# Six of the first pair's sixteen on-chip moves put on ScalarE's queue, and the remainders of the last two combinations of x put on VectorE, the last combination started after the first scores

## The chip, the cores and the metric

The kernel runs on one core of one Trainium2 chip. The metric is device time in microseconds (us), of one launch that computes both layers. Times of single instructions come from a profile of one execution.

## What is computed

The reference is a two-layer encoder block over x of shape (1, 512, 1024), in float32. Each layer is RMSNorm, one input projection, a token mixer with per-head RMS-normed queries and keys, a product with silu(gate), an output projection and a residual add.

```python
def reference(x, ...):
    for i in range(DEPTH):                       # 2 layers
        hn = rms_norm(x, norm_gain[i])
        if i % 2 == 0:
            y = mixer_a(hn, a_w_in, a_w_out, a_q_gain, a_k_gain, t5_bias)
        else:
            y = mixer_b(hn, b_w_in, b_w_out, b_q_gain, b_k_gain, b_rpb)
        x = x + y

def mixer_a(hn, w_in, w_out, q_gain, k_gain, t5_bias):
    proj = hn @ w_in                             # 1024 -> 3 groups * (q, k, v) * 1024, and a gate
    for g, (window, dilation) in enumerate(((128, 1), (512, 4), (2048, 16))):
        o, lse = dilated_group_attention(rms_norm(q), rms_norm(k), v, bias, dilation, reach)
    y = sum over g of softmax(lse)[g] * o[g]     # the three groups share one softmax
    return (y * silu(gate)) @ w_out
```

`mixer_b` is neighbourhood attention on an 8 x 64 grid. The change touches layer A alone, and in it the first pair of heads and the preparation of x.

## The kernel before

**Matrix products.** Every float32 operand is split into a high part that TensorE takes in its fast float32 form (`..._h`, `wh`) and a remainder (`..._l`, `wl` = value minus high part); a product is three matmuls. ScalarE makes the high parts of the weights (`cast`), VectorE and GpSimd take turns at the remainders (`rest`). Weights come through eight `wraw` buffers, and there are six `wh` and five `wl` buffers.

**Layer A's projections.** The sixteen heads are worked in eight pairs, `hc` = 0 to 7. Pairs 1 to 7 form their projections with fewer products, as in Strassen's scheme: `main_a(hc)` multiplies quarters of x with four sums of weight blocks, and, for that, four combinations of the quarters of x are made once, in `mix()`. `mix()` makes combination n in three steps (`put(n, ...)`): a VectorE sum or difference into the buffer `mixed`, a ScalarE copy into `mix_h[:, n]`, and a subtraction into `mix_l[:, n]`, on the engine that `put` is given. All are [128 x 1024]. They are made in the order 0, 1, 3, 2, and the products of `main_a` ask for them in that order too (`yield "mix", n`). Combination 2 is used last, behind the second scores of the first pair.

**Attention of a pair** is `attn_a(hc)`. `scores(u)`, u = 0 and 1, gives four [128 x 512] tiles each; `least` puts on each a VectorE minimum, a ScalarE exponential (`exponents`), a ScalarE scaling (`normalise`) and a VectorE transposition into `pq` (`turn`; buffer name `pt`). When the eight tiles of the pair are in `pq`, sixteen DMAs of 64 KB move [32 x 512] blocks from `pq` to another buffer, `t0` (also printed `pt`), in which the rows stand in the order that the local group's product needs: `move(n)`, n = 0 to 3, issues four of them, all on SyncE's queue. Each reads columns that all eight transpositions write. `weigh()` then gives the output `o` in 128 small matmuls `o<-pt,rawk`, which read `pq` itself, and 64 matmuls `o<-pt,v`, which read `t0` and so wait for the moves. `weighed` multiplies it with the gate.

**Order.** TensorE's order is written out by hand. A main stream of products and a side stream of attention work are interleaved by a planner's clock, `clock`, in ns: it adds up what each matmul should take (213 ns for 512 columns). `yield "wait", key, delay` holds the side stream until that clock is `delay` past the time put into `stamp[key]`; `yield key` makes the main stream run the side stream until the key is there; `later_on(delay, job)` sets work off when the clock has gone on by `delay`. Inside `in_order()`, and in `keep_in_program_order(...)`, work keeps the written order on its engine; the rest of VectorE's, ScalarE's, GpSimd's and SyncE's order comes from a scheduler at build time. At run time each engine works off its own list strictly in order, and a DMA that SyncE issues waits, at the head of SyncE's list, for its data.

Around the change the order by the planner's clock is: `put(3)` at 47.8 us, `put(2)` at 52.9, keys transposed (`k_a(0)`) from 61.0, first scores at 64.5, second scores at 74.9, moves from 84.7 to 88.6, `weigh` at 93.5.

Of the kernel before, what the change touches and what calls it, by code (L numbers as in the profile page):

```python
# [13 lines left out]
F32 = mybir.dt.float32  # L14
# [8 lines left out]
P = 128  # L23
# [3 lines left out]
NHC = 8  # L27
# [19 lines left out]
def tile_hybrid_encoder(  # L47
# [19 lines left out]
    wk = ctx.enter_context(tc.tile_pool(name="wk", bufs=2))  # L67
# [22 lines left out]
    @contextmanager  # L90
    def in_order():

        was, held[0] = held[0], True
        yield
        held[0] = was

    vec, act, pol, syn = (Ordered(e) for e in (nc.vector, nc.scalar, nc.gpsimd, nc.sync))

    def sb(t, off, dims):
        return bass.AP(t.tensor, t.offset + off, [t.ap[0]] + dims)  # L100
# [13 lines left out]
    def bank(name):  # L114

        return ps_side.tile([P, 512], F32, tag="side", name=name)
# [18 lines left out]
    mix_h = big.tile([P, 4, 4, H], F32R, tag="yh", name="mix_h")  # L135
    mix_l = big.tile([P, 4, 4, H], F32R, tag="yl", name="mix_l")
# [180 lines left out]
    stamp = {("qk", -1): 0, ("w", -1): 0}  # L317
# [26 lines left out]
    def later_on(delay, job):  # L344

        timers.append((clock[0] + delay, job))
        timers.sort(key=lambda t: t[0])
# [120 lines left out]
    pq = wk.tile([P, 4096], F32, tag="pt", name="pt", bufs=1)  # L468
# [57 lines left out]
    def mix():  # L526


        x11, x12, x21, x22 = (x_all[:, k : k + KH, t : t + H] for t in (0, H) for k in (0, KH))
        t = wk.tile([P, 2, KH, H], F32, tag="tr", name="mixed", bufs=1)  # L530
        a, b = t[:, 0], t[:, 1]

        def put(n, out, op, x, y, eng):
            with in_order():
                op(out, x, y)
                act.copy(mix_h[:, n], out)
                eng.tensor_sub(mix_l[:, n], out, mix_h[:, n].bitcast(F32))
            stamp["mix", n] = 0

        yield "wait", ("first",), 500  # L540
        yield from first_out()
        yield 1500
        put(0, a, vec.tensor_sub, x21, x22, pol)
        yield 2000
        put(1, b, vec.tensor_sub, a, x11, vec)
        yield 2000
        yield from bias_lines()
        yield "wait", ("rawk", 0), 1000
        put(3, b, vec.tensor_add, b, x12, pol)
        yield 5000  # L550
        put(2, a, vec.tensor_sub, x11, x21, pol)

    def row_sums(ssq):

# [5 lines left out]
    def bias_lines():  # L560

        oh = wk.tile([32, 896], F32, tag="k12", name="oh", bufs=1)
        tc.keep_in_program_order(syn.dma_start(oh, onehot))
        t5 = wk.tile([32, 48], F32, tag="e0", name="t5", bufs=1)
        syn.dma_start(t5, t5t)
        mk = wk.tile([16, 896], F32, tag="q12", name="mk", bufs=1)
        syn.dma_start(mk, maskc)
        yield 3000
        for g, (o, n) in enumerate(((0, 384), (384, 256), (640, 256))):
            pl = bank("pl")  # L570
            matmul(pl[0:16, :n], t5[:, 16 * g : 16 * g + 16], oh[:, o : o + n], start=True, stop=True)
            vec.tensor_sub(mk[:, o : o + n], mk[:, o : o + n], pl[0:16, :n])
        for j in range(4):
            syn.dma_start(l0_d[:, j, j : j + 384], mk[:, 0:384])
        syn.dma_start(l12_d, mk[:, 384:896])
        yield
# [77 lines left out]
    def first_out():  # L654

        raw, ss = st.pop("first")
        for i in range(4):
            t = raw[:, i, :]
            act.activation(t, t, AF.Copy, scale=rs_n[:, i : i + 1])
            squares(t, ss, i, 8)  # L660
            yield 0
        normed(raw, ss, 8, "rawq", 0)
# [242 lines left out]
    class turner:  # L905
# [7 lines left out]
        def put(self, src, n, off):  # L913

            dst = sb(self.t, off, [[32, n // P], [self.run, 4], [1, 32]])
            vec.transpose(dst, src[:, :n].rearrange("p (i b k) -> p i b k", b=4, k=32))
# [21 lines left out]
    def attn_a(hc):  # L938
# [1 line left out]
        q0h, q0l, q12, k0h, k0l = st.pop(("q", hc))  # L940
        k12, v12 = st.pop(("k12", hc))
        last = hc == NHC - 1
        t0 = pq if last else wk.tile([P, 2048], F32, tag="tr", name="pt0", bufs=1)
        run = 1024 if last else 512
        moved = []
        at = lambda t, hd: 32 * (4 * hd + t)
# [4 lines left out]
            src = pr[:, 512 - P * n : 512]  # L951
            vec.transpose(dst, src.rearrange("p (i b k) -> p i b k", b=4, k=32))

        def move(n):

            place = t0.rearrange("p (a x) -> p a x", a=4)
            for b in range(4):
                a = (b + n) % 4
                src = pq[32 * a : 32 * a + 32, 1024 * b : 1024 * b + 512]
                tc.keep_in_program_order(syn.dma_start(place[32 * b : 32 * b + 32, a, :], src))  # L960
            moved.append(n)
            if len(moved) == 4:
                stamp["pt", hc] = clock[0]

        def scores(u):

            tiles = []
            for t in (2 * u, 2 * u + 1):
                cs, n = (64, 192) if t == 0 else (0, 192) if t == 3 else (0, 256)
                tiles.append((t, [bank("log") for _ in range(2)], cs, n))  # L970
            for t, lgs, cs, n in tiles:
                ks = slice(P * t + cs, P * t + cs + n)
                qs = slice(P * t, P * t + P)
                mm3_heads(
                    [lg[:, cs : cs + n] for lg in lgs],
                    lambda hs: q0h[hs, qs], lambda hs: q0l[hs, qs],
                    lambda hs: k0h[hs, ks], lambda hs: k0l[hs, ks], False,
                )
            for t, lgs, cs, n in tiles:
                for g in range(2):  # L980
                    for j in range(4):
                        c = P * t + 32 * j
                        for hd in range(2):
                            hs = slice(64 * hd, 64 * hd + 64)
                            matmul(
                                lgs[hd][32 * j : 32 * j + 32, 256 + P * g : 384 + P * g],
                                q12[hs, g, c : c + 32],
                                by_class(k12[hs, g, :])[:, :, j],
                                share=2,
                                start=False,  # L990
                                stop=(g == 1),
                            )
            return [(hd, t, lgs[hd], cs, n) for t, lgs, cs, n in tiles for hd in range(2)]
# [43 lines left out]
        def weigh():  # L1037
            os, v0 = [bank("o") for _ in range(4)], st.pop("v0")
            mms = []
            for g in range(2):  # L1040
                for b in range(4):
                    for j in range(4):
                        own = slice(32 * j, 32 * j + 32)
                        c, d = P * g, 1024 * b + 256 * (2 + g)
                        mms.append((
                            lambda hs, j=j: os[j][hs, :P],
                            lambda hs, own=own, b=b, c=c: v12[own, b, c + hs.start : c + hs.stop],
                            lambda hd, own=own, d=d: pq[own, d + at(0, hd) : d + at(0, hd) + P],
                        ))
            for i in range(4):  # L1050
                (ta, ia), (tb, ib) = ((i - 1, 1), (i, 0)) if i else ((0, 0), (3, 1))
                n, m = 32 * (tb - ta), 256 * (ib - ia) + 32 * (tb - ta)
                for a in range(4):
                    mms.append((
                        lambda hs, a=a, d=32 * ta, n=n: sb(os[a][hs], d, [[n, 2], [1, 32]]),
                        lambda hs, i=i: v0[:, i, hs],
                        lambda hd, d=run * a + 256 * ia + 32 * ta, m=m: sb(t0, d + 128 * hd, [[m, 2], [1, 32]]),
                    ))
            yield from side_by_side(mms, 4)
            return os  # L1060

        if last:
# [21 lines left out]
            for c in range(4):  # L1084
                src = gt.rearrange("p (t ja x) -> p x ja t", t=4, ja=8)[:, 4 * c : 4 * c + 4]
# [15 lines left out]
        for u in range(2):  # L1101
            for n, tile_ in enumerate(scores(u)):
                later_on(400 + 900 * n, partial(least, n, tile_))
            if u:
                stamp["scored", hc] = 0
                for n in range(4):
                    later_on(8000 + (2000 if hc else 1300) * n, partial(move, n))
            yield 8500
        fill = bias_rows() if hc == 2 else None
        yield from v_a(hc)  # L1110
        yield "wait", ("pt", hc), 2500
        if hc:
            st["e", hc + 1] = bias_a(hc + 1)
        yield "wait", ("pt", hc), (4500, 11500)[hc] if hc < 2 else 9000 if hc == NHC - 2 else 7500
        yield "wait", ("gate", hc), 4000
        gt = weighed(hc, (yield from weigh()))
        if not hc:
# [402 lines left out]
```

## Time and profile before

| | us |
|---|---|
| median of 3 runs | 858.39 (854.2 to 860.99) |
| the profiled execution, its own time | 856.92 |
| its span | 855.1 |
| TensorE matmul busy | 833.6 (97%) |
| VectorE busy | 634.5 (74%) |
| ScalarE busy | 507.5 (59%) |
| GpSimd busy | 296.5 (35%) |

Engines are called PE (TensorE's matmuls), PEld (its weight loads), DVE (VectorE), ACT (ScalarE), POOL (GpSimd) and SP (SyncE); SPq and ACTq are their DMA issues. A row of a timeline has the start in us, the duration in us, the engine, the line, the operation, what it writes and reads, the form, the count, and in brackets how long the engine had been idle and what ended that. Matmuls are pipelined, so the pace is the distance between starts, not the printed duration. L324 and L328 are the lines of the helpers that record matmuls and transpositions, L85 that of all other engines' work.

### The profile page before, as it was taken

The page shows a single profiled execution, that of the slowest core. Times are in us where ns is not written, and L with a number is a line of the kernel's source. Part 1 is how long each engine was busy: PE and PEld are TensorE (multiplying, and loading weights), DVE is VectorE, ACT ScalarE, POOL GpSimd, SP SyncE. Part 2 cuts the span into 40 slices and gives each one's busy share as a digit, 9 for nine tenths or more (in the row PEclk, how much of TensorE's full clock was granted, in tenths as well). Part 3 has the DMA queues.
Part 4 walks back from the last instruction along what each step waited for, and adds up shares of the span by engine and source line. Part 5 has one row for each costly group of instructions (what it writes and reads, how often), then busy time and mean ns, then how long its engine had stood idle before and what let it go on. Part 6 is the DMA issues. An engine that isn't in the chain of part 4 may idle for free.

```text
span 855.1 us, 18125 instructions
## 1 busy us (share of the span) xinstructions
PE 833.6 (97%) x6611; PEld 688.8 (81%) x6611; DVE 634.5 (74%) x1653; ACT 507.5 (59%) x1066; POOL 296.5 (35%) x259
## 2 busy tenths in 40 slices
PE   9998989999999999999999999899999999999998
PEld 6876867878877878878877877689998898889786
DVE  7899895797897787786886866656578666776742
ACT  7566665765855846846846828545456654665440
POOL 5045442362453543543533514113123322322301
PEclk9999999999999999999999999999999999999999
DMA  9425754766676775776675664283264456534212
GB/s 339 138 56 134 206 130 136 144 164 193 136 174 193 159 176 180 161 164 184 157 174 178 126 193 144 80 297 112 81 193 145 124 169 185 158 134 126 84 50 99
DMA packets 56169, 131.97 MB, mean 154 GB/s; under 512 B 7184, under 2 KB 24528, under 8 KB 55952
## 3 DMA queue, kind: packets, MB, share of 16 engines
q1 hardware_dynamic: 49744, 108.78, 40.5%
q0 software_dynamic: 6048, 22.02, 15.0%
q8 instruction: 52, 0.85, 0.4%
q14 instruction: 37, 0.30, 0.1%
q10 hardware_dynamic: 288, 0.01, 0.0%
HBM read 111.73 MB, written 11.72 MB: 144 GB/s over the span
## 4 chain that ended last, share of the span: by engine, by line
PE 70%; ACT 10%; DVE 10%; DMA 5%; issue 3%; SPq 1%; POOL 1%; ACTq 0%; DVEq 0%
PE acc L324 58%; ACT p L85 4%; PE log L324 4%; PE o L324 4%; DMA wraw<-in_w 3%; PE tp L328 3%; DVE wl L85 2%; ACT wh L85 2%; SPq L85 1%; ACT rawk L85 1%; DVE rawq L85 1%; DVE na L85 1%; DMA e<-l_d 1%; DVE p L85 1%; DVE gt L85 1%
## 5 line engine op out<-in xcount | busy, mean ns | idle before, releaser
L85 POOL TENSOR_TENSOR wl<-wraw,wh 128x512 fp32r<-128x512 f32 (+1 forms) x153 | 197.4, 1291 | 425.2 <-PE acc L324 200.2
L85 ACT CAST wh<-wraw 128x512 fp32r<-128x512 f32 (+1 forms) x360 | 209.7, 593 | 198.9 <-PE acc L324 158.2
L85 DVE TENSOR_TENSOR wl<-wraw,wh 128x512 fp32r<-128x512 f32 (+1 forms) x207 | 160.4, 778 | 43.3 <-PE acc L324 33.9
L324 PE MATMUL acc<-wh,hn_h 128*128 128x384 f32 (+1 forms) x488 | 186.7, 383 | 3.0 <-DVE gt L85 1.7
L324 PE MATMUL acc<-wl,hn_h 128*128 128x384 f32 (+1 forms) x488 | 177.5, 364 | 0.4 <-DVE wl L85 0.4
L324 PE MATMUL acc<-wh,hn_l 128*128 128x384 f32 (+1 forms) x488 | 177.5, 364 | 0.0
L85 ACT ACTIVATE p<-p,mn 128x256 f32<-128x256 f32 (+2 forms) x248 | 137.7, 584 | 32.1 <-DVE mn L85 32.1
L324 PEld LDWEIGHTS acc<-wh,hn_h 128*128 128x128 f32 x488 | 92.3, 189 | 21.6 <-issue 6.8
L324 PEld LDWEIGHTS acc<-wh,hn_l 128*128 128x128 f32 x488 | 92.1, 189 | 9.8
L324 PEld LDWEIGHTS acc<-wl,hn_h 128*128 128x128 f32 x488 | 92.6, 190 | 8.5 <-DVE wl L85 1.1
L324 PE MATMUL acc<-wl,mix_h 128*128 128x512 f32 x224 | 88.2, 394 | 2.1 <-DVE wl L85 2.1
L324 PE MATMUL acc<-wh,mix_h 128*128 128x512 f32 x224 | 89.5, 400 | 0.0
L324 PE MATMUL acc<-wh,mix_l 128*128 128x512 f32 x224 | 87.8, 392 | 0.0
L324 PE MATMUL acc<-hn_h,wh 128*128 128x512 f32 x192 | 79.0, 412 | 0.3 <-ACT rawb L85 0.2
L324 PE MATMUL acc<-hn_h,wl 128*128 128x512 f32 x192 | 75.1, 391 | 0.0
L324 PE MATMUL acc<-hn_l,wh 128*128 128x512 f32 x192 | 75.0, 391 | 0.0
L85 DVE STREAM_TRANSPOSE pt<-p 128x512 f32<-128x512 f32 (+1 forms) x60 | 40.6, 687 | 23.7 <-ACT p L85 23.6
L85 DVE TENSOR_REDUCE ss<-sq 128x4 f32<-128x256 f32 (+1 forms) x96 | 46.1, 500 | 11.1 <-POOL sq L85 5.9
L324 PE MATMUL acc<-y_h,wh 128*128 128x512 f32 x128 | 51.9, 405 | 0.5 <-ACT gt L85 0.5
L324 PEld LDWEIGHTS acc<-wl,mix_h 128*128 128x128 f32 x224 | 42.3, 189 | 11.5 <-DVE wl L85 3.3
L324 PEld LDWEIGHTS acc<-wh,mix_h 128*128 128x128 f32 x224 | 42.2, 188 | 10.0 <-issue 1.6
L324 PE MATMUL acc<-y_h,wl 128*128 128x512 f32 x128 | 50.0, 391 | 0.0
(149 smaller groups left out, 1379.8 us busy)
## 6 DMA issues: line engine op xcount, KB each, us to landing
wraw<-in_w SPq DMA_DIRECT2D x95, 512.0 KB
wraw<-in_w POOLq DMA_DIRECT2D x42, 512.0 KB, 7.0
wraw<-in_w SPq DMA_DIRECT2D x38, 384.0 KB
pt<-pt SPq DMA_DIRECT2D x112, 64.0 KB
td<-tr SPq DMA_DIRECT2D x24, 224.0 KB
pt<-td SPq DMA_DIRECT2D x24, 224.0 KB
e<-l_d SPq DMA_DIRECT2D x32, 112.0 KB
e<-l_d SPq DMA_DIRECT2D x16, 128.0 KB
```

The source lines that it names most:

```text
L85: m = f(*args, **kw)
L324: nc.tensor.matmul(o, l, r, **kw)
L328: nc.tensor.transpose(o, i, ident)
```

## The change

`put` is given a delay: with it, the remainder is taken that much later by the planner's clock. The remainders of combinations 3 and 2 go from GpSimd (`pol`) to VectorE (`vec`), 1500 and 3000 ns behind their combination. Combination 2, the last, starts 15000 ns behind combination 3. Because it still uses `mixed` then, the buffer `t0`, which shares its place, is taken at the first move only.

`move` takes a queue and a list of blocks. For the first pair (`hc` = 0) ten of the sixteen moves stay on SyncE's queue, at 8000 to 11000 ns behind the second scores, and six go on ScalarE's, at 12000 to 16500 ns. For the other pairs all stay on SyncE's, with the times as they were. The waits ahead of the first pair's `weigh`, 2500 and then 4500 ns behind the last move, become zero.

```diff
-        def put(n, out, op, x, y, eng):
+        def put(n, out, op, x, y, eng, wait=0):
+            def split():
+                with in_order():
+                    eng.tensor_sub(mix_l[:, n], out, mix_h[:, n].bitcast(F32))
+                stamp["mix", n] = 0
+
             with in_order():
                 op(out, x, y)
                 act.copy(mix_h[:, n], out)
-                eng.tensor_sub(mix_l[:, n], out, mix_h[:, n].bitcast(F32))
-            stamp["mix", n] = 0
+            later_on(wait, split) if wait else split()
...
-        put(3, b, vec.tensor_add, b, x12, pol)
+        put(3, b, vec.tensor_add, b, x12, vec, 1500)
+        later_on(15000, partial(put, 2, a, vec.tensor_sub, x11, x21, vec, 3000))
         yield 5000
-        put(2, a, vec.tensor_sub, x11, x21, pol)
...
-        t0 = pq if last else wk.tile([P, 2048], F32, tag="tr", name="pt0", bufs=1)
+        t0 = [pq] if last else []
...
-        def move(n):
-
-            place = t0.rearrange("p (a x) -> p a x", a=4)
-            for b in range(4):
+        def move(n, queue, bs):
+
+            if not t0:
+                t0.append(wk.tile([P, 2048], F32, tag="tr", name="pt0", bufs=1))
+            place = t0[0].rearrange("p (a x) -> p a x", a=4)
+            for b in bs:
                 a = (b + n) % 4
                 src = pq[32 * a : 32 * a + 32, 1024 * b : 1024 * b + 512]
-                tc.keep_in_program_order(syn.dma_start(place[32 * b : 32 * b + 32, a, :], src))
-            moved.append(n)
-            if len(moved) == 4:
+                tc.keep_in_program_order(queue.dma_start(place[32 * b : 32 * b + 32, a, :], src))
+                moved.append(a)
+            if len(moved) == 16:
                 stamp["pt", hc] = clock[0]
+
+        def moves():
+            if hc:
+                for n in range(4):
+                    later_on(8000 + 2000 * n, partial(move, n, syn, range(4)))
+                return
+            for n in range(4):
+                later_on(8000 + 1000 * n, partial(move, n, syn, (0, 2, 3) if n % 2 else (1, 3)))
+            for i, (n, b) in enumerate(((0, 0), (0, 2), (1, 1), (2, 0), (2, 2), (3, 1))):
+                later_on(12000 + 900 * i, partial(move, n, act, (b,)))
...
-                for n in range(4):
-                    later_on(8000 + (2000 if hc else 1300) * n, partial(move, n))
+                moves()
...
-        yield "wait", ("pt", hc), 2500
+        yield "wait", ("pt", hc), 2500 if hc else 0
         if hc:
             st["e", hc + 1] = bias_a(hc + 1)
-        yield "wait", ("pt", hc), (4500, 11500)[hc] if hc < 2 else 9000 if hc == NHC - 2 else 7500
+        yield "wait", ("pt", hc), (0, 11500)[hc] if hc < 2 else 9000 if hc == NHC - 2 else 7500
```

More of the change, by code (lines that the diff above doesn't have):

```diff
@@ L1056, in weigh @@
                         lambda hs, i=i: v0[:, i, hs],
-                        lambda hd, d=run * a + 256 * ia + 32 * ta, m=m: sb(t0, d + 128 * hd, [[m, 2], [1, 32]]),
+                        lambda hd, d=run * a + 256 * ia + 32 * ta, m=m: sb(t0[0], d + 128 * hd, [[m, 2], [1, 32]]),
                     ))
```

## The prediction

> **What bounds the kernel now.** I read the page first, then TensorE's waits, then the timeline of each engine around the waits that stand out.
>
> ```profile
> span 855.1 us, 18125 instructions
> PE 833.6 (97%) x6611; PEld 688.8 (81%) x6611; DVE 634.5 (74%) x1653; ACT 507.5 (59%) x1066; POOL 296.5 (35%) x259
> ```
>
> TensorE bounds the kernel: it is idle for 855.1 - 833.6 = 21.5 us in all. A change that leaves the matmuls alone, as this one does, can win only from those 21.5 us and from stretches in which TensorE runs at a lower clock. Its waits between 40 and 140 us, the stretch that the change touches, are these:
>
> ```profile
> PE o L324 <- DMA e<-l_d: 2.8, 1, 2.8
> PE acc L324 <- DVE wl L85: 2.1, 1, 2.1
> PE o L324 <- DMA pt<-pt: 1.0, 1, 1.0
> PE tp L328 <- DVE k0l L85: 0.9, 1, 0.9
> PE tp L328 <- ACT vt L85: 0.2, 1, 0.2
> ```
>
> That makes 7.0 us, a third of all idle time, in two places: ahead of the first scores (0.9 and 2.1) and ahead of `o<-pt,v`, which needs the moves (2.8 and 1.0; the name in the first is only the DMA that ended last). The timeline of TensorE, with the windows of its clock, shows that each place costs more than its wait:
>
> ```profile
> 77.63 0.63 PE L328 MATMUL tp<-ident,rawk 128*128 128x128 f32 x4 [0.88 <-DVE k0l L85]
> 81.32 0.50 PE L324 MATMUL acc<-wl,mix_h 128*128 128x512 f32 x1 [2.14 <-DVE wl L85]
> 82.34 0.60 PE L324 MATMUL acc<-wh,mix_h 128*128 128x512 f32 x1
> 85.00 0.53 PE L324 MATMUL log<-k0h,q0h 64*128 64x192 f32 x2
> 87.44 0.50 PE L324 MATMUL acc<-wh,mix_h 128*128 128x512 f32 x1
> 97.19 0.38 PE L324 MATMUL log<-k0h,q0h 64*128 64x256 f32 x2
> 99.17 0.50 PE L324 MATMUL acc<-wh,mix_h 128*128 128x512 f32 x1
> 106.59 0.39 PE L324 MATMUL acc<-wh,mix_l 128*128 128x512 f32 x1
> 125.28 0.39 PE L324 MATMUL acc<-wh,hn_l 128*128 128x512 f32 x1
> 128.50 0.59 PE L324 MATMUL o<-pt,v 128*64 128x64 f32 x8 [2.83 <-DMA e<-l_d]
> 130.06 3.06 PE L324 MATMUL o<-pt,v 128*64 128x64 f32 x56 [0.97 <-DMA pt<-pt]
> 133.06 0.80 PE L324 MATMUL acc<-wh,hn_h 128*128 128x512 f32 x1
> 193.56 2.08 PE L324 MATMUL o<-pt,v 128*64 128x64 f32 x64
> ```
>
> ```profile
> 84.00:86.00 2.00, 2.00 (x12) 0.51 1.03 254
> ```
>
> (In the window: matmul busy time, their count, granted clock, DMA share, GB/s.) Behind the first place the clock is at about half. Six matmuls from 82.34 to 85.00 take 2.66 us; undisturbed, 32 steps from 99.17 to 106.59 take 7.42 us, 0.232 each, so six take 1.39. The first scores take 87.44 - 85.00 = 2.44 us, the second, undisturbed, 99.17 - 97.19 = 1.98. **First place:** 0.88 + 2.14 + (2.66 - 1.39) + (2.44 - 1.98) = 4.75 us. **Second place:** from the end of the row at 125.28, 125.67, to 133.06 are 7.39 us; the next pair's same 64 matmuls take 2.08: 5.31 us. Together 10.06 us is what there is to win.
>
> **Part one, the combinations.** The first place in the other engines:
>
> ```profile
> 75.07 1.05 ACT L85 CAST mix_h<-mixed 128x1024 fp32r<-128x1024 f32 x1 [1.18 <-DVE mixed L85]
> 76.02 0.68 ACT L85 ACTIVATE k0h<-tp,gk 128x512 fp32r<-128x512 f32 x1
> 83.28 0.74 ACT L85 ACTIVATE k<-tp,gk 128x512 f32<-128x512 f32 x1
> 88.44 0.62 ACT L85 CAST wh<-wraw 128x512 fp32r<-128x512 f32 x1 [3.92 <-PE acc L324]
> 71.72 8.99 POOL L85 TENSOR_TENSOR mix_l<-mixed,mix_h 128x1024 fp32r<-128x1024 f32 x2 [8.28 <-ACT mix_h L85]
> 73.82 1.22 DVE L85 TENSOR_TENSOR mixed<-pt 128x1024 f32<-128x1024 f32 x1
> 78.42 2.85 DVE L85 TENSOR_TENSOR wl<-wraw,wh 128x512 fp32r<-128x512 f32 x1
> 88.44 0.69 DVE L85 TENSOR_TENSOR rawq<-acc,rawk 128x512 f32<-128x512 f32 x1 [2.55 <-PE acc L324]
> 78.00:84.00 6.00, 3.86 (x17) 2.66 (x16) 6.00 (x6) 6.00 (x14) 4.87 (x4) 0.88 0.41 80
> L85 POOL TENSOR_TENSOR mix_l<-mixed,mix_h x3: 2554/2804/6483, 52.8 to 78.2; 128x1024 fp32r<-128x1024 f32 x3
> L85 DVE TENSOR_TENSOR mix_l<-mixed,mix_h x1: 1211/1211/1211, 59.6 to 59.6; 128x1024 fp32r<-128x1024 f32 x1
> ```
>
> (The last two rows are groups: shortest, median and longest in ns, first and last start. The row ahead of them is a window: busy time of PE, PEld, DVE, ACT and POOL, granted clock, DMA share, GB/s.) TensorE's 2.14 us go back to the VectorE remainder `wl` at 78.42: it takes 2.85 us, where a subtraction of twice its width takes 1.21 (last row), so some 0.6 would do, while GpSimd works through both remainders of the combinations from 71.72 to 80.71. The two engines hinder each other: GpSimd's one takes 6.48 us and its other 2.55. The 0.88 us go back to `k0l`, which waits for `k0h` on ScalarE; that stands behind the copy of combination 2 at 75.07, for which ScalarE was idle for 1.18 us waiting for VectorE's difference.
>
> What is removed here: 8.99 us of GpSimd; on ScalarE the copy at 75.07 and the idle time ahead of it (76.02 - 75.07 + 1.18 = 2.13 us earlier for `k0h` and all behind it); on VectorE the difference at 73.82 (1.22). What is added here: combination 3's remainder on VectorE, 1.21. VectorE's load is thus the same, without the some 2.2 us that its `wl` lost. `k0h` ends 2.1 us earlier, more than the 0.88, and the `wl` at 78.42 comes some 3 us earlier, more than the 2.14: both waits go, and the low clock with them. What is late next: the scores need the key copies on ScalarE, the last at 83.28 to 84.02. ScalarE is full there (6.00 of 6 us from 78 to 84), so its chain moves by the 2.13 us, to 81.9; the scores, 4.75 us earlier, run from 80.25 to 82.7, and the part that reads the keys is their second half. I take off 0.35 and count **4.4 us**. Bounds: nothing but the 2.14 us less VectorE's 1.21, so 0.9, if the order of ScalarE's work stays as hindering as now, and 4.75.
>
> What is moved to behind the first scores: one difference (1.22), one copy (1.05), one remainder (1.21). By the planner's clock they come at 47.8 + 15.0 = 62.8 and 3 us later, the first scores at 64.5 (85.00 in the trace). There VectorE is idle for 2.55 us and ScalarE for 3.92 (rows at 88.44): the cover is 2.55 against 2.43 on VectorE, so I cost it at nothing. If it goes, the minima of the first scores come up to 2.4 us later, and, since VectorE is nearly full up to the last transposition, so do the moves. Combination 2 is wanted 15.5 us of the planner's clock behind its start; I see no wait in that. GpSimd's weight sums by DMA, queued behind the two remainders until 80.7, come earlier, which costs nothing.
>
> **Part two, the moves.** Their chain:
>
> ```profile
> 113.50 11.74 SPq L85 DMA_DIRECT2D pt<-pt  x16
> 124.63 5.39 DMA pt<-pt
> 118.00:120.00 2.00, 2.00 (x69) 1.64 (x68) 1.97 (x4) 0.08 (x1) 0.00 (x0) 1.00 0.32 80
> 126.00:128.00 2.00, 0.00 (x0) 1.00 1.06 223
> 114.00 1.05 ACT L85 COPY vt<-acc 128x512 f32<-128x512 f32 x1
> 124.04 0.42 ACT L85 ACTIVATE sq<-rawk 128x256 f32<-128x256 f32 x1 [5.96 <-DVE rawk L85]
> 0.74 0.41 ACTq L85 DMA_DIRECT2D ng<-in_norm_gain  x1
> 183.92 10.64 SPq L85 DMA_DIRECT2D e<-l_d  x6
> ```
>
> The last transposition lets SyncE start at 113.50; sixteen issues take 11.74 us, 0.734 each; the last lands at 124.63 + 5.39 = 130.02. In the window from 118 to 120 the DMA engines are busy for 0.32 only: it is the issuing that holds up the moves there, not the transfer. The trace shows no issue of such a block on ScalarE; the nearest rows are its two small loads (0.41) and SyncE's 112 KB loads, 10.64 / 6 = 1.77 each in a crowded stretch. I take SyncE's 0.734 for the same block.
>
> Ten issues end at 113.50 + 7.3 = 120.8, six on ScalarE cost 4.4 us of its list. ScalarE is busy until 118.08 and idle for 5.96 us behind that (row at 124.04): the 4.4 fit, and the casts that slip are made ahead into six `wh` buffers, 6 x 6 x 0.232 = 8.4 us of matmuls. The sixth leaves by about 121. Landing takes between 3 us (an estimate: 64 KB blocks under a DMA share of a third instead of 1.06) and 5.39: 124 to 126.4, against 125.67, where TensorE gets there. I take off 0.5 us for that and 0.2 for the copies of `vt`: TensorE already waits 0.2 us for them, and the first ScalarE move is planned about where they are. The planned place of `weigh` hardly moves (11.9 + 4.5 = 16.4 us behind the scores before, 16.5 + 0 now). All of this rides on what part one wins; both shift alike. So **4.6 us** of 5.31; bounds: 5.3 - 13.7 = -8.4 (the slower rival below) and 5.3. Weight loads behind the moves on SyncE's queue leave 4.4 us earlier, about as much as TensorE is earlier.
>
> A rule speaks against this part: the Trainium skill, page "DMA: Bandwidth & Descriptors", section "Issuing engines are not separate DMA queues", says that DMAs of several engines run on the same 16 DMA engines and interleave, so that a second issuing engine saves the sequencer's issue time alone, usually small beside the transfer. By it this part would win next to nothing; the windows above, 0.32 busy while the queue issues, say that here the issue is the larger part.
>
> **The sum.** 4.4 + 4.6 = 9.0 us. The profiled execution took 856.92, 1.5 under the median of the three runs; the mean of all four is 857.6, which I start from: 857.6 - 9.0 = **848.6 us**, 1.1% under the median of 858.39. A measurement of this kernel tells about 1% from no change.
>
> **The rivals.** (B) The transfer is the limit: from 126 to 128 the DMA share is 1.06, with weight sums and loads that the shorter SyncE queue now lets in earlier. The sixth move then lands 4 us late and only 0.6 us of part two is left: 857.6 - 4.4 - 0.6 = 852.6. This is what the page's rule comes to. For it: the 5.39 us of the last move. Against: the share of 0.32 before. (C) The first place gives its time back: VectorE or ScalarE, both full from 78 to 84, make TensorE wait at the scores, or the minima wait for combination 2. Then 0.9 + 4.0 is left: 852.7. For it: their full rows; against: 2.13 us less on ScalarE. (D) Slower. ScalarE's list is worked strictly in order; the six moves each stand at its head until the last transposition is done and the issue is through. If they come ahead of the `vt` copies at 114.00 and cost what the crowded issues cost, 6 x 1.77 = 10.6, plus 1.5 us of waiting for the transposition, TensorE waits 12 us for `vt`, and again 1.7 at low clock; 857.6 - 4.4 - 5.3 + 13.7 = 861.6, and up to 868 when the casts behind fall short too. It decides from about 8 us of standing on. For it: ScalarE is busy up to 118.08, and TensorE's wait for `vt`. Against: issues of these very blocks took 0.734. (E) The change doesn't do what it says: the scheduler, which orders what isn't kept in order, puts other work in the gaps, and waits come back behind. 857.6.
>
> **How the numbers follow.** Forecast 0.60, B 0.11, C 0.09, D 0.15, E 0.05. The forecast's own range is 845 to 852. Faster by over 1% (under 849.8): 0.51, of the forecast's 0.60. Slower by over 1% (over 867): the upper part of D and a part of it that I can't price, 0.13. Within 1%: 0.36. The range that holds the time 8 times in 10 takes in B, C, E and the lower half of D: 844 to 862.
>
> **What would show it.** Right: no GpSimd `mix_l` behind 60 us; `wl` of 0.7 us around 78; `k0h` at 74; no wait of TensorE over 0.5 us and a granted clock of 1.0 from 76 to 88; ten moves on SyncE in some 7.3 us and six on ScalarE; `o<-pt,v` in about 2 us; the row that stood at 133.06 at about 124. Wrong: a clock of 0.5 ahead of the first scores, `tp<-ident,vt` waiting for several us, or moves that land 5 us after their issue with TensorE idle.

## The result and the profile after

The changed kernel takes 847.61 us (median of 4 runs, 845.44 to 848.36), the kernel before beside it 858.38 (854.20 to 860.99): a ratio of 0.9881 with a 95% interval of 0.9842 to 0.9919. It was run again later, beside the kernel before: 0.9900 (0.9879 to 0.9922). The time lies 1 us under the predicted 848.6, inside its range of 845 to 852.

TensorE's waits between 40 and 140 us, after (engine, line, what it waited for: us in total, times, longest):

```profile
PE acc L324 <- DVE wl L85: 1.3, 1, 1.3
PE tp L328 <- ACT vt L85: 0.8, 1, 0.8
```

Before there were 7.0 us in five rows; now there are 2.1 in two. Both waits ahead of `o<-pt,v` are gone, those for `k0l` and for `wl` at 81 us too; a wait for `wl` of 1.3 us stands at a new place, and the one for `vt` has grown from 0.2 to 0.8. The page:

```profile
span 846.3 us, 18123 instructions
PE 828.1 (98%) x6611; PEld 684.9 (81%) x6611; DVE 631.6 (75%) x1655; ACT 507.8 (60%) x1066; POOL 289.2 (34%) x257
```

TensorE's idle time fell from 21.5 to 846.3 - 828.1 = 18.2 us, and its busy time by 5.5 for the same 6611 matmuls. Of these 5.5, 3.2 are the low clock of the two places, which is gone (1.27 + 0.46 and 5.31 - 3.80 by the prediction's rows). Another 1.3 lie in the first 20 us, ahead of the change: the trace shows waiting there instead, and TensorE is at the same work at 67.5 us in both. The rest was not traced. Its timeline after, at the rows shown of before:

```profile
67.50 0.60 PE L328 MATMUL tp<-ident,rawq 128*128 128x128 f32 x4
73.57 0.49 PE L324 MATMUL acc<-wl,hn_h 128*128 128x512 f32 x1 [1.32 <-DVE wl L85]
78.06 0.60 PE L328 MATMUL tp<-ident,rawk 128*128 128x128 f32 x4
81.79 0.36 PE L324 MATMUL log<-k0h,q0h 64*128 64x192 f32 x2
83.79 0.50 PE L324 MATMUL acc<-wh,mix_h 128*128 128x512 f32 x1
112.26 0.66 PE L328 MATMUL tp<-ident,vt 128*128 128x128 f32 x4 [0.80 <-ACT vt L85]
122.47 2.09 PE L324 MATMUL o<-pt,v 128*64 128x64 f32 x64
124.49 0.50 PE L324 MATMUL acc<-wh,hn_h 128*128 128x512 f32 x1
```

The first scores start at 81.79 instead of 85.00 and take 2.00 us instead of 2.44; the 64 matmuls that read the moves take 2.09 in one piece; the matmul behind them starts at 124.49 instead of 133.06. Those 8.57 us are nearly all of the 855.1 - 846.3 = 8.8 us of span: what follows hands the time on. The other engines there, after:

```profile
71.69 1.23 DVE L85 TENSOR_TENSOR mix_l<-mixed,mix_h 128x1024 fp32r<-128x1024 f32 x1 [0.45 <-ACT mix_h L85]
72.83 0.68 DVE L85 TENSOR_TENSOR wl<-wraw,wh 128x512 fp32r<-128x512 f32 x1
77.44 0.68 DVE L85 TENSOR_TENSOR wl<-wraw,wh 128x512 fp32r<-128x512 f32 x1
81.55 1.21 DVE L85 TENSOR_TENSOR mixed<-pt 128x1024 f32<-128x1024 f32 x1
85.40 1.21 DVE L85 TENSOR_TENSOR mix_l<-mixed,mix_h 128x1024 fp32r<-128x1024 f32 x1
```

```profile
73.80 0.68 ACT L85 ACTIVATE k0h<-tp,gk 128x512 fp32r<-128x512 f32 x1
110.22 0.60 ACTq L85 DMA_DIRECT2D pt<-pt  x1
110.86 1.06 ACT L85 COPY vt<-acc 128x512 f32<-128x512 f32 x1
114.54 0.53 ACTq L85 DMA_DIRECT2D pt<-pt  x1
120.69 0.42 ACT L85 ACTIVATE sq<-rawk 128x256 f32<-128x256 f32 x1 [5.25 <-DVE rawk L85]
110.21 7.37 SPq L85 DMA_DIRECT2D pt<-pt  x10
```

(The last row is SyncE's queue.) `k0h` stands at 73.80 instead of 76.02, no `wl` is held for 2.85 us, and combination 2 goes in around the first scores: it doesn't start behind them, as the title says, but at 81.55, just ahead of them, and its remainder at 85.40 comes behind. Ten issues on SyncE's queue end at 117.58; the six on ScalarE's run from 110.22 to 115.07, 0.52 to 0.60 each (two of them shown), and ScalarE's idle time behind them is still 5.25 us.

For what follows I cut TensorE's timeline into two stretches: from the first transposition of `rawq` to the first scores (first place), and from there to the first matmul behind `o<-pt,v` (second place). The first row of before is this one; the others stand in the prediction:

```profile
67.51 0.60 PE L328 MATMUL tp<-ident,rawq 128*128 128x128 f32 x4
```

Before: 85.00 - 67.51 = 17.49 and 133.06 - 85.00 = 48.06. After: 14.29 and 42.70. In the second profile of the changed kernel they are 14.27 and 42.68, so they repeat far better than the times of whole runs do.

### The profile page after: what moved, and what is told of

Same layout as the page of the kernel before. It is cut to its first block, busy times and chain, and to the rows that moved or that the text cites. A ratio compares the mean times of both kernels' runs of the same rounds, so it can differ in the third digit from the quotient of the medians.

```text
span 846.3 us, 18123 instructions
## 1 busy us (share of the span) xinstructions
PE 828.1 (98%) x6611; PEld 684.9 (81%) x6611; DVE 631.6 (75%) x1655; ACT 507.8 (60%) x1066; POOL 289.2 (34%) x257
## 4 chain that ended last, share of the span: by engine, by line
PE 71%; ACT 10%; DVE 8%; DMA 5%; issue 3%; SPq 2%; POOL 1%; DVEq 0%; ACTq 0%
PE acc L324 59%; PE log L324 4%; ACT p L85 4%; DMA wraw<-in_w 4%; PE o L324 4%; PE tp L328 3%; ACT wh L85 2%; DVE wl L85 2%; SPq L85 2%; ACT rawk L85 1%; DVE na L85 1%; DMA pt<-in_xt 1%; DVE gt L85 1%; POOL sq L85 1%; DVE p L85 1%
## 5 line engine op out<-in xcount | busy, mean ns | idle before, releaser
L85 DVE TENSOR_TENSOR wl<-wraw,wh 128x512 fp32r<-128x512 f32 (+1 forms) x207 | 156.9, 761 | 42.9 <-PE acc L324 32.9
L324 PE MATMUL acc<-y_l,wh 128*128 128x512 f32 x128 | 49.9, 390 | 0.0
```

Source lines behind the costliest of these rows:

```text
L85: m = f(*args, **kw)
L324: nc.tensor.matmul(o, l, r, **kw)
```

## The experiments

The theory (A): the two parts remove two separate waits of TensorE. The first is a matter of VectorE's and ScalarE's order ahead of the first scores, the second of how fast sixteen DMAs can be issued on one queue. All kernels ran in three sets, each on one chip beside the kernel before: the combinations alone, the moves alone, all sixteen on SyncE and six ahead of `vt` in the first; the changed kernel again, the two on combination 2 and the first run of both small edits in the second; the rest in the third. Medians compare best within a set. The table has the ratio with its 95% interval, and the two stretches of each profile in us.

| kernel | median us | ratio to before | first stretch | second |
|---|---|---|---|---|
| before | 856.26, 857.80, 855.40 beside the three sets | 1 | 17.49 | 48.06 |
| changed, again | 848.82 | 0.9900 (0.9879 to 0.9922) | 14.27 | 42.68 |
| combinations alone | 854.44 | 0.9970 (0.9946 to 0.9993) | 14.29 | 49.16 |
| moves alone | 850.81 | 0.9925 (0.9899 to 0.9952) | 17.84 | 42.29 |
| all sixteen on SyncE | 855.60 | 0.9982 (0.9962 to 1.0001) | 14.29 | 49.05 |
| three on ScalarE | 850.09 | 0.9926 (0.9900 to 0.9953) | 14.27 | 43.45 |
| six ahead of `vt` | 853.64 | 0.9959 (0.9941 to 0.9976) | 14.28 | 48.22 |
| combination 2 at once, VectorE | 852.87 | 0.9947 (0.9928 to 0.9966) | 15.91 | 44.27 |
| combination 2 late, GpSimd | 849.67 | 0.9910 (0.9889 to 0.9930) | 13.10 | 45.49 |
| remainder of 3 later | 848.64 | 0.9914 (0.9889 to 0.9939) | 13.07 | 43.59 |
| ScalarE moves behind `vt` | 846.78 | 0.9894 (0.9865 to 0.9922) | 14.29 | 42.66 |
| both of these | 847.51, again 846.74 | 0.9892 (0.9868 to 0.9917), 0.9898 (0.9871 to 0.9925) | 13.06, 13.07 | 43.67, 43.64 |

**The combinations alone.**

```diff
-                later_on(8000 + 1000 * n, partial(move, n, syn, (0, 2, 3) if n % 2 else (1, 3)))
-            for i, (n, b) in enumerate(((0, 0), (0, 2), (1, 1), (2, 0), (2, 2), (3, 1))):
-                later_on(12000 + 900 * i, partial(move, n, act, (b,)))
+                later_on(8000 + 1300 * n, partial(move, n, syn, range(4)))
...                                     # waits ahead of weigh 2500 and 4500 again
```

> Only the change to the combinations (remainders of 3 and 2 on VectorE, combination 2 behind the first scores); all sixteen moves on SyncE's queue at the old times, old waits ahead of weigh. Theory A (the two parts act in two places and add up): the first place wins 3.5 to 4 us as in the changed kernel, the second place is back with 5 us of waiting and low clock: 852.5 to 854, that is 4.5 to 6 us slower than the changed kernel. Rival B (the combinations alone bring most, since all that follows shifts): within 2 us of the changed kernel, 848 to 850. Rival C (the time won at the first place is given back at the moves): as before the change, 856 to 858.

The first stretch has all of its gain (14.29), but the second is 1.10 us longer than before the change. A part is given back: between A and C. The place, in TensorE's and SyncE's timelines of this kernel, and then its last move in the chain of waits (start, us, what):

```profile
125.06 0.34 PE L324 MATMUL o<-pt,v 128*64 128x64 f32 x4 [2.83 <-issue]
126.54 0.34 PE L324 MATMUL o<-pt,v 128*64 128x64 f32 x4 [1.15 <-DMA pt<-pt]
127.63 3.25 PE L324 MATMUL o<-pt,v 128*64 128x64 f32 x56 [0.75 <-DMA pt<-pt]
110.07 12.08 SPq L85 DMA_DIRECT2D pt<-pt  x16
```

```profile
121.56 6.03 DMA pt<-pt
```

The issues start 3.43 us earlier (113.50 before), but take 12.08 instead of 11.74 and the last lands in 6.03 instead of 5.39, at 127.59: 2.43 us earlier than before. TensorE is 3.35 us earlier at the scores; ahead of `o<-pt,v` it waits 4.73 us here and waited 3.80 before.

**The moves alone.**

```diff
-        put(3, b, vec.tensor_add, b, x12, vec, 1500)
-        later_on(15000, partial(put, 2, a, vec.tensor_sub, x11, x21, vec, 3000))
+        put(3, b, vec.tensor_add, b, x12, pol)
         yield 5000
+        put(2, a, vec.tensor_sub, x11, x21, pol)
```

> Only the change to the moves (six on ScalarE's queue, waits of zero ahead of weigh); the combinations as before, on GpSimd and at once. Theory A: the first place is as before (a wait of 2.1 us for wl, 0.9 for k0l, half clock behind), the second is gone: 852.5 to 854. Rival B: the moves bring little by themselves, 856 to 858. Rival C: the moves bring nearly all, 848 to 850.

Under A's range at 850.81: the first stretch is nearly as before (17.84), the second 42.29, all won. By the stretches the combinations alone win 17.49 + 48.06 - 14.29 - 49.16 = 2.10 us and the moves alone 5.42, together 7.52; both at once win 8.56. The missing 1.04 is what the combinations lose when the moves are slow: the parts help each other.

**All sixteen on SyncE's queue**, at the changed kernel's planned times.

```diff
-                later_on(12000 + 900 * i, partial(move, n, act, (b,)))
+                later_on(12000 + 900 * i, partial(move, n, syn, (b,)))
```

> The changed kernel with the six moves at the same planned times but on SyncE's queue, so that only the queue is undone; waits, combinations and order of the matmuls stay. Theory A (the issue on one queue, 0.73 us each, was the limit): sixteen issues again take 11 to 12 us, TensorE waits 3 to 4 us ahead of o<-pt,v, and 5 us are lost: 852 to 854. Rival B (the shorter waits and the earlier planned moves did it): 847 to 849, as the changed kernel. Rival C (transfer is the limit, so where they are issued doesn't matter): also 847 to 849.

Timelines of TensorE and SyncE, and then, from the chain of waits, two slow issues and the last move (start, us, what):

```profile
126.85 3.68 PE L324 MATMUL o<-pt,v 128*64 128x64 f32 x64 [4.85 <-DMA pt<-pt]
109.83 12.07 SPq L85 DMA_DIRECT2D pt<-pt  x16
```

```profile
118.42 1.04 SPq L85
119.50 1.75 SPq L85
121.30 5.41 DMA pt<-pt
```

With nothing undone but the queue, the second stretch loses 49.05 - 42.70 = 6.35 us: 4.85 of waiting and 3.68 - 2.09 = 1.59 of half clock. B (the shorter waits ahead of `weigh`) and C (transfer is the limit) fall. The time is at 855.60 above A's range.

**Three of the six back on SyncE's queue.**

```diff
-                later_on(12000 + 900 * i, partial(move, n, act, (b,)))
+                later_on(12000 + 900 * i, partial(move, n, syn if i % 2 == 0 else act, (b,)))
```

> The changed kernel with three of the six ScalarE moves back on SyncE's queue: thirteen there, three on ScalarE's. With sixteen on one queue TensorE waited 4.85 us ahead of o<-pt,v and ran those 64 matmuls at half clock (3.7 instead of 2.1 us); with ten none. Theory A (the last issue on the queue sets the end, 0.73 us for each move): thirteen end 2.2 us earlier than sixteen, so the wait is 2 to 3 us, less if the landing is quicker too; 850 to 852. Rival B (congestion at the time of landing is what counts, from 120 us on, when GpSimd's weight sums start): the last move still lands in it, a wait of 3.5 to 5 us, 853 to 855. Rival C (the landing is quick as soon as the queue is a little shorter): a wait under 1 us, 847.5 to 849.

The same views of this kernel:

```profile
122.76 2.17 PE L324 MATMUL o<-pt,v 128*64 128x64 f32 x64 [0.75 <-DMA pt<-pt]
109.83 8.61 SPq L85 DMA_DIRECT2D pt<-pt  x13
```

```profile
117.85 4.77 DMA pt<-pt
```

The wait is 0.75 us: taking three moves off the queue removes 4.10 of the 4.85 us. Thirteen issues take 8.61 us, 0.66 each, instead of 0.75 (sixteen in 12.07), and the landing 4.77 instead of 5.41. The last issue ends at 118.44 here and at 121.90 there, so 3.46 of the 4.10 us are issue time; TensorE gets to `o<-pt,v` at about 122.0 in both. It isn't one price for each issue, as A had it: in the chain of the kernel with sixteen most issues take 0.59 us, but two of the last three 1.04 and 1.75 (above), and thirteen are through ahead of those. C's wait is right, though the time at 850.09 lies above C's range and in A's.

**All six ahead of the `vt` copies in ScalarE's list.**

```diff
-                later_on(12000 + 900 * i, partial(move, n, act, (b,)))
+                later_on(8000 + 500 * i, partial(move, n, act, (b,)))
```

> The changed kernel with the six ScalarE moves planned 4 to 6.5 us earlier, which puts all six ahead of the vt copies in ScalarE's list, where the changed kernel has one. Theory A (an issue stands for 0.6 us in ScalarE's list, and TensorE's transposition of vt waits for it): the wait for vt grows from 0.8 us by five issues, 3 us, to 3.5 to 4 us, and some of it is given back ahead of o<-pt,v, which no longer waits: 850 to 852.5. Rival D of the prediction (crowded issues of 1.77 us, and standing until the last transposition): a wait of 9 to 12 us, 858 or more. Rival E (ScalarE's issues cost its list nothing, as they run beside its arithmetic): 847.5 to 848.5.

Timelines of ScalarE and TensorE, and a window of TensorE (busy time, granted clock, DMA share, GB/s):

```profile
110.45 2.72 ACTq L85 DMA_DIRECT2D pt<-pt  x4
113.29 1.18 ACTq L85 DMA_DIRECT2D pt<-pt  x2
114.51 1.08 ACT L85 COPY vt<-acc 128x512 f32<-128x512 f32 x1 [0.63 <-issue]
115.92 1.11 PE L328 MATMUL tp<-ident,vt 128*128 128x128 f32 x4 [4.23 <-ACT vt L85]
```

```profile
116.00:118.00 2.00, 2.00 (x7) 0.50 0.42 101
```

The mechanism of rival D is real: issues ahead of the `vt` copy hold it up. The copy starts 3.65 us later than in the changed kernel (0.24 of it because the whole trace stands that much later), TensorE waits 4.23 us instead of 0.80, and runs at a clock of 0.50 behind it. The second stretch loses 5.52 us, and the time at 853.64 lies above A's range: A's sum had the wait, but not the clock behind it. D's wait of 12 us is refuted: six issues take 3.9 us, 0.65 each and not 1.77.

**Deferral and engine of the combinations, apart.** First the deferral undone, both remainders on VectorE:

```diff
-        later_on(15000, partial(put, 2, a, vec.tensor_sub, x11, x21, vec, 3000))
         yield 5000
+        put(2, a, vec.tensor_sub, x11, x21, vec, 3000)
```

> The changed kernel with combination 2 at its old place, 5 us behind combination 3, but both remainders on VectorE: only the deferral is undone. Theory A (two causes: GpSimd's hold on VectorE made the 2.1 us, ScalarE's copy of combination 2 ahead of k0h the 0.9 us): the wait for wl stays small, the one for k0l is back, since the copy stands ahead of k0h again, and VectorE's extra 2.4 us come ahead of the scores: 1.5 to 3 us slower than the changed kernel. Rival B (the deferral is all of it): 3.5 to 4.5 us slower. Rival C (the engine is all of it): within 1 us of the changed kernel.

ScalarE, VectorE and TensorE in this kernel's timeline:

```profile
76.34 1.05 ACT L85 CAST mix_h<-mixed 128x1024 fp32r<-128x1024 f32 x1 [2.86 <-DVE mixed L85]
78.00 0.75 DVE L85 SCALAR_TENSOR_TENSOR k0l<-tp,gk,k0h 128x512 fp32r<-128x512 f32 x1 [0.77 <-ACT k0h L85]
78.90 0.63 PE L328 MATMUL tp<-ident,rawk 128*128 128x128 f32 x4 [0.88 <-DVE k0l L85]
84.25 0.38 PE L324 MATMUL log<-k0h,q0h 64*128 64x256 f32 x1 [0.66 <-ACT k L85]
85.34 0.38 PE L324 MATMUL log<-k0h,q0h 64*128 64x256 f32 x1 [0.71 <-ACT k L85]
```

Then the engine undone, at the new times on GpSimd:

```diff
-        put(3, b, vec.tensor_add, b, x12, vec, 1500)
-        later_on(15000, partial(put, 2, a, vec.tensor_sub, x11, x21, vec, 3000))
+        put(3, b, vec.tensor_add, b, x12, pol, 1500)
+        later_on(15000, partial(put, 2, a, vec.tensor_sub, x11, x21, pol, 3000))
```

> The changed kernel with the remainders of 3 and 2 on GpSimd at the new times: only the engine is undone. Theory A: combination 3's remainder on GpSimd from 71.7 hinders VectorE or is hindered by it until 76 to 78, and a wl on VectorE is held for up to 2 us; the 1.3 us wait for wl that the changed kernel has, behind its VectorE remainder, goes: from 1 us faster to 2 us slower than the changed kernel. Rival B (the deferral is all): within 1 us. Rival C (the engine is all): 3 to 4 us slower, with the 2.1 us wait back.

GpSimd and VectorE in this kernel's timeline:

```profile
71.71 5.37 POOL L85 TENSOR_TENSOR mix_l<-mixed,mix_h 128x1024 fp32r<-128x1024 f32 x1 [8.29 <-ACT mix_h L85]
82.57 1.93 POOL L85 TENSOR_TENSOR wl<-wraw,wh 128x512 fp32r<-128x512 f32 x1
82.05 3.54 DVE L85 TENSOR_TENSOR mixed<-pt 128x1024 f32<-128x1024 f32 x1
```

Both hold parts of A, and their sizes differ. The engine alone wins 17.49 - 15.91 = 1.58 us in the first stretch: the wait of 2.14 for `wl` is gone, but ScalarE's copy stands ahead of `k0h` again, with 2.86 us of idle time ahead of it, and the 0.88 us are back. In the second stretch the scores then wait 0.66 and 0.71 us for ScalarE's key copies. This kernel is 4.05 us slower than the changed one beside it, B's range and not A's 1.5 to 3.

The deferral alone wins 4.39 us in the first stretch, more than the changed kernel: both old waits are gone, since combination 2's remainder on GpSimd has moved away from the `wl` that it held up as well. Its second stretch is 2.8 us longer than the changed kernel's. One cause in the trace: VectorE's difference for combination 2 takes 3.54 us instead of 1.21 beside a weight remainder of GpSimd that starts at 82.57. The changed kernel has that remainder too, at 82.53, but its difference starts 0.5 us earlier, at 81.55, and is done by 82.76. So a part of the 2.8 is how two pieces of work happen to fall together; how large a part was not tried. In time this kernel is 0.85 us slower than the changed one, inside A's range and B's.

Both stretches together are 60.13 us with the moves alone, 60.18 with the engine on top, 58.59 with the deferral on top and 56.99 with both. So the engine by itself gains nothing, the deferral by itself 1.54 us and both 3.14. In the first stretch the deferral is all of the gain; what the engine adds lies behind the first scores.

**Two small edits on top.** The remainder of combination 3 at 5000 instead of 1500, the ScalarE moves behind the `vt` copies, and both:

```diff
-        put(3, b, vec.tensor_add, b, x12, vec, 1500)
+        put(3, b, vec.tensor_add, b, x12, vec, 5000)
...
-                later_on(12000 + 900 * i, partial(move, n, act, (b,)))
+                later_on(13500 + 600 * i, partial(move, n, act, (b,)))
```

> The changed kernel with only combination 3's remainder later (5000 instead of 1500 ns behind it). Theory A: the wait of 1.3 us for wl at 73.6 goes and 0.5 us of it comes back at the key copies ahead of the scores: 0.5 to 1.3 us faster than the changed kernel. Rival B: nothing, because the time comes back at vt or at the moves.

> The changed kernel with only the ScalarE moves later (from 13500, 600 apart), all behind the vt copies. Theory A: TensorE's wait for vt falls from 0.8 us by at most 0.6, the issue that stood ahead of it: 0.1 to 0.6 us faster than the changed kernel, at the edge of what can be told. Rival B: the moves land later and TensorE waits ahead of o<-pt,v: slower by 1 us or more.

> A version that might beat the changed kernel: combination 3's remainder 5000 instead of 1500 ns behind it, and the ScalarE moves from 13500 on, 600 apart, all behind the vt copies. Theory A: TensorE's wait of 1.3 us for wl at 73.6 goes, and its wait for vt falls from 0.8 to 0.5, so 1.0 to 1.6 us faster, if the moves still land before TensorE is there: 846 to 847. Rival B (VectorE is full up to the scores, so the wait only moves to a later wl or to k0l): as the changed kernel. Rival C (the later moves land late): a wait ahead of o<-pt,v of 1 us or more, 848 to 851.

> The version with both edits (combination 3's remainder later, ScalarE moves behind vt) once more, beside its two halves: 846 to 848, 1.0 to 1.4% under the kernel before; if the halves add up, their gains against the changed kernel make up its own.

The first edit removes the 1.3 us wait at 73 us and shortens the first stretch by 1.22, but the second is 0.9 longer; 0.57 us of that is a wait of the scores for ScalarE's key copies (TensorE's timeline of the kernel with the first edit):

```profile
82.92 0.38 PE L324 MATMUL log<-k0h,q0h 64*128 64x256 f32 x1 [0.57 <-ACT k L85]
```

The first edit leaves 56.66 us for both stretches against the changed kernel's 56.99. The second edit changes them by 0.04, with a wait for `vt` of 0.63 instead of 0.80, and both together leave 56.73 and 56.71. The first run of both, at 847.51, lies above its A's 846 to 847. The gain left of the first edit is 0.33 us, nearer to B than to A. The ratios of all four runs lie inside the changed kernel's own two intervals: no version was shown to beat it.

**The changed kernel, again.**

> The changed kernel once more, so that it stands on the same chip beside the next three and beside the kernel before: 846.5 to 848.5, 1.0 to 1.3% under the kernel before. If the kernels with the moves on one queue are the ones that scatter (8 to 9 us between their runs so far), it spreads over less than 4 us.

It stayed in its range by the ratio and came out at 848.82, a little above by the time. Its six runs span 3.1 us. The scatter of others isn't tied to the one queue, as that text supposed: of the two kernels with one queue one spans 8.75 us, the other 5.88 and not 8 to 9, and the kernel with combination 2 at once has its moves on two queues and spans 5 us.

## Why the prediction was right

**What there was to win.** 10.06 us were counted; 8.57 were won by TensorE's timeline, against 9.0 forecast. The waits, the low clock behind them and the two places were read rightly, and the signs that the prediction named all came. Its sum had one limit too few: the new wait stands at 73.57, ahead of the stretch from 76 to 88 that it looked at.

**First place.** Forecast 4.4 us; measured 85.00 - 81.79 = 3.21 and 0.44 of clock in the scores, 3.65. The mis-sized step is "VectorE's load is thus the same": it is, but combination 3's remainder stands at 71.69, earlier than the difference that left 73.82, waits there 0.45 us for ScalarE at the head of VectorE's list, and holds up the `wl` behind it, which TensorE then wanted. That cost 1.32 us, and moving the remainder removed it. The forecast saw the next limit, ScalarE's key copies, at 0.35 us; it appears at 0.57 as soon as that wait is gone.

**Its cause** was named only in part. GpSimd holding up VectorE's `wl` and the copy ahead of `k0h` are the two causes of the old waits, as the prediction read them. But the deferral by itself removes both: with both remainders still on GpSimd but combination 2 late, this place won 4.39 us. With both on VectorE and combination 2 at once it won 1.58, since the 0.88 stays and the 1.3 us for combination 3's remainder is new. So the new engine was not needed at this place, and combination 3's remainder on VectorE cost time there.

**Second place.** Forecast 4.6 us; measured 8.57 - 3.65 = 4.92. The moves land in time, so the 0.5 us taken off for landing weren't needed; the wait for `vt` grew by 0.6 instead of 0.2. ScalarE's issues cost 0.52 to 0.60 instead of the assumed 0.734. That the one queue held up the moves was shown by undoing it alone: 6.35 us. With thirteen on it instead of sixteen, 3.46 of 4.10 us came from the earlier end of the issues and 0.64 from a quicker landing; so it is the issue in the main, and a landing of about 5 us stays on the path behind it. The Trainium skill ("DMA: Bandwidth & Descriptors", section "Issuing engines are not separate DMA queues") says that a second issuing engine saves only the sequencer's time to start the DMA, which is usually small beside the DMA itself. That it is the issue time in the main agrees with these runs; that it is small does not, and there the measurement decides: sixteen blocks of 64 KB take 12 us to issue on one queue, beside landings of 5 to 6.

**The rivals.** B (transfer is the limit) fell: the moves land before TensorE is there. C (the first place gives its time back) did not come in the changed kernel, where the scores don't wait; its mechanism shows in two others, with waits of 1.37 and 0.57 us for ScalarE's key copies. D's mechanism is there, but with all six issues ahead of `vt` it cost 5.52 us and not 13.7; the changed kernel avoids it by the order of ScalarE's list. E fell with the waits. The chances don't fit D's price: 861.6 is within 1% of 858.39, yet nearly all of D was counted as over 867.

**Luck.** The errors of the two terms, -0.75 and +0.32, partly cancel, which makes the total look better than its parts. The two medians differ by 10.8 us, with 7 to 13.6 by the interval, the two profiled spans by 8.8; that the time came within 1 us is partly luck as well.

## What to carry to other kernels

Price a wait of TensorE with the slow clock behind it, and read what stands at the head of the other engines' lists at that moment: one early combination that nobody needed yet made two waits here, by its copy ahead of a needed one and by its remainder on an engine that hindered VectorE. Starting it later removed both; another engine by itself gained nothing. When many small DMAs are released by one event, compare the time of the issues with the DMA share. Here, with the DMA engines a third busy while one queue issued, splitting the list over two queues was worth the issue time and the slow clock behind the wait. Put such issues behind whatever the issuing engine owes TensorE.

## What the runs showed of the hardware

Between 40 and 140 us, waits of TensorE of 2.1 to 4.85 us were followed by a granted clock near 0.5; waits of up to 1.49 us (for `vt`, in the kernel with combination 2 late on GpSimd) were not. Windows of TensorE (busy time, granted clock, DMA share, GB/s), the first behind the wait of 2.1 us in the kernel with the moves alone, the second behind that of 1.32 in the changed kernel:

```profile
82.00:84.00 2.00, 2.00 (x8) 0.50 0.82 109
```

```profile
74.00:76.00 2.00, 2.00 (x12) 1.00 0.25 74
```

The Trainium skill ("TensorE: Matmul & The Clock Gate", "HAM oscillation — how this bites in real kernels") asks for no idle gaps above about 3.4 us. The measurement here is stricter, and it decides for this kernel: with the moves alone, a wait of 2.12 us with one of 0.87 some 4 us ahead of it was enough. Whether the shorter one counts was not tried:

```profile
77.76 0.63 PE L328 MATMUL tp<-ident,rawk 128*128 128x128 f32 x4 [0.87 <-DVE k0l L85]
81.44 0.80 PE L324 MATMUL acc<-wl,mix_h 128*128 128x512 f32 x1 [2.12 <-DVE wl L85]
```

A DMA issue of the same 64 KB took 0.75 us on average in a list of sixteen, 0.66 in one of thirteen and 0.68 to 0.74 in lists of ten, all on SyncE's queue, and 0.51 to 0.84 on ScalarE's. In the chains of waits most issues on SyncE's queue take 0.58 to 0.60 us; the averages differ by single slow ones, such as the two at 118.42 and 119.50 above. The mean busy share of the DMA engines in that kernel rises from 0.72 (118 to 120 us) to 1.07 (120 to 122); whether that is the reason was not tried.
